# Hyena filter spectra by one radix-2 step, stored once per group, and buffers of their own for the last modulation tiles

## The chip, the cores and the metric

The kernel runs on one core of a Trainium2 chip. The metric is the device time of one execution in microseconds; lower is better. Five engines of the core matter here: TensorE (PE in the profile, its weight loads PEld), VectorE (DVE), ScalarE (ACT), GpSimd (POOL) and SyncE (SP), which here only issues transfers.

## The reference, cut to what matters

Two layers of a diffusion backbone on 256 latent and 256 context tokens of width 2048: an even layer (state-space group and attention group side by side), an odd layer with a Hyena convolution, each with a feed-forward part. Every sub-layer is modulated by vectors that come from `c` (latent) and `c_ctx` (context) through large matrices. The Hyena convolution uses two long filters per channel, which depend on parameters only: a small sine network gives `hid`, and

```python
h_two = jnp.einsum('lf,fkd->lkd', hid, fw_out[:, i]) * window[:, None, :]
k = jnp.concatenate([h_two[:, 0], jnp.zeros((1, d)), jnp.flip(h_two[1:, 1], axis=0)], axis=0)
k = k / jnp.sum(jnp.abs(k), axis=0, keepdims=True)
kf = jnp.fft.rfft(k, axis=0)
uf = jnp.fft.rfft(u, n=2 * seq_len, axis=1)
return jnp.fft.irfft(uf * kf, n=2 * seq_len, axis=1)[:, :seq_len]
```

The kernel computes the spectra `kf` of both filters and the sums of absolute values before anything else, and keeps the spectra in device memory (`kscr`) for the odd layer.

## The kernel before, in words

A TensorE product that must keep full precision is made of three: an operand is cut into a rounded high half (a copy on ScalarE, line 347) and a low half (a subtraction on VectorE, line 348) by `split`, and `mm3` issues high×high, low×high and high×low (lines 380 to 382). Weights come as `raw` tiles of 1 MB and are cut into `whi` and `wlo` in this way.

Only the start of the program is touched. `startup` runs four generators, each of which gives way at every `yield`; `turn` always takes the one whose count of turns, divided by its entry in `START_RATE`, is lowest. Which engine gets what in which order is set by that alone: each engine works off its own queue in program order, and each transfer stands in the queue of the engine that issues it. The four are:

- `filters`: loads the tables, runs the three sine layers (`sin`, `hid`) and forms `hs` and `hd`, the token sums and differences. Then eight groups `gi`: 512 channels of one of the two filters each. A group multiplies by the output weights `fw` (12 products into `pss`), multiplies by the decay window (`sv`, line 762, VectorE), splits that (`sh`, `sl`), takes absolute values (line 766, ScalarE) and their maximum (`am`, line 768), sums over tokens by products with a column of ones (`psl`, 16 of them), and takes a reciprocal into `kinv`. Four blocks of 128 frequencies follow: six `psk` products each over the 256 tokens, an eviction by ScalarE into `ko` (line 785, three buffers of 256 KB) and a store of 256 KB into `kscr`, which ScalarE's own queue issues (line 786).
- `on_pe`: the modulation vectors that layer 0 needs first. 32 tiles `mraw` of 1 MB from `modn` (line 1360), each with eight products into `ps_mod`; after each four tiles a copy `row`, eight small transposing products `ps_modT`, and short column work on VectorE (`mcol`, `mctx`, lines 1375 and 1378) with the scaling of `x` and `cin` (line 1383).
- `stats(0)` and `stats(1)`: loads of the latent and the context tokens, sums of squares (ScalarE, then accumulation on VectorE, line 498) and the reciprocal norm.

When `filters` is through, its pool is closed, the `act` tile is laid out, and `halves` forms the normed inputs (lines 1431 and 1432, `act`) of the four column groups whose modulation is complete. Then the rest of `on_pe`, the first loads of `w_in` (`fetch`, line 352), and layer 0's first projection tasks (`acc` products). The other modulation matrices (`mod`, line 446, 160 tiles) are loaded and used along the whole program: `run` adds to `mod_debt` with each task and loads one tile whenever it reaches 1; VectorE forms each tile's product with `cb` (line 453, 128×2048).

## Time and profile before

| | us |
|---|---|
| median of 3 runs | 2681.16 (2681.15 to 2690.86) |
| profiled execution | 2686.52 |
| its span on the core | 2684.7 |
| mean granted clock of TensorE | 0.992 |

The profiled execution is 5.36 us above the median, and 1.8 us of it lie outside the span. All times of the trace are microseconds from the span's start.

### The profile page before, as it was taken

How to read it: one execution, taken by the hardware profiler on the slowest of the kernel's cores; microseconds unless marked ns; L12 is line 12 of the kernel's file. 1: busy time of each engine (PE TensorE's matmuls, PEld its weight loads, DVE VectorE, ACT ScalarE, POOL GpSimd, SP SyncE). 2: the span in 40 equal slices, each digit the busy share in tenths (PEclk: the TensorE clock that was granted, in tenths of full speed). 3: DMA queues.
4: the chain of work that ended last, by engine and by line, in shares of the span. 5: the costliest groups of instructions: out<-in, count | busy, mean ns of one | idle time of the engine just before them, and what ended most of it. 6: DMA issues, size and time to landing. Idle time of an engine off the chain costs nothing.

```text
span 2684.7 us, 39715 instructions
## 1 busy us (share of the span) xinstructions
PE 2621.0 (98%) x15320; PEld 2241.7 (83%) x15320; DVE 2070.8 (77%) x3137; ACT 1438.6 (54%) x2313; POOL 0.9 (0%) x10
## 2 busy tenths in 40 slices
PE   5999999999999999999999999999999999999998
PEld 2557778988898888888888888888988888888887
DVE  6458776967798888887989999998888656656656
ACT  4463564656564544444546755555654544544545
POOL 0000000000000000000000000000000000000000
PEclk9999999999999999999999999999999999999999
DMA  8776546746578988887887554555578654655543
GB/s 330 271 263 236 197 165 218 260 144 249 205 289 309 334 309 297 320 330 282 341 314 283 199 179 167 189 183 211 205 284 286 211 188 162 215 174 188 201 157 129
DMA packets 108861, 635.88 MB, mean 237 GB/s; under 512 B 11648, under 2 KB 20224, under 8 KB 48256
## 3 DMA queue, kind: packets, MB, share of 16 engines
q1 hardware_dynamic: 104064, 624.95, 64.9%
q10 hardware_dynamic: 4608, 8.39, 0.8%
q8 instruction: 121, 1.98, 0.3%
q14 instruction: 68, 0.56, 0.1%
HBM read 622.81 MB, written 10.49 MB: 236 GB/s over the span
## 4 chain that ended last, share of the span: by engine, by line
PE 89%; DMA 4%; DVE 4%; ACT 1%; issue 1%; SPq 0%; DVEq 0%; ACTq 0%
PE acc L569 40%; PE acc L570 22%; PE acc L813 7%; PE acc L572 3%; PE acc L380 2%; PE acc L381 2%; PE acc L382 2%; DMA mraw<-in_mod 2%; DMA kscr<-ko 1%; PE ps_mod L1363 1%; DVE wlo L348 1%; PE ps_c L380 1%; PE ps_c L382 1%; PE ps_c L381 1%; ACT whi L347 1%
## 5 line engine op out<-in xcount | busy, mean ns | idle before, releaser
L569 PE MATMUL acc<-act,whi 128*128 128x512 f32 x3525 | 1256.8, 396 | 3.0 <-ACT whi L347 3.0
L348 DVE TENSOR_TENSOR wlo<-raw,whi 128x1024 fp32r<-128x1024 f32 (+1 forms) x842 | 937.2, 1118 | 236.3 <-ACT whi L347 229.8
L347 ACT ACTIVATE whi<-raw 128x1024 fp32r<-128x1024 f32 (+1 forms) x842 | 814.3, 972 | 465.4 <-PE acc L569 245.7
L570 PE MATMUL acc<-act,wlo 128*128 128x256 f32 x3760 | 1022.5, 282 | 1.5 <-DVE wlo L348 1.4
L569 PEld LDWEIGHTS acc<-act,whi 128*128 128x128 f32 x3525 | 666.6, 189 | 149.3 <-ACT whi L347 3.8
L570 PEld LDWEIGHTS acc<-act,wlo 128*128 128x128 f32 x3760 | 710.5, 189 | 23.2 <-DVE wlo L348 3.4
L569 PE MATMUL acc<-hh,whi 128*128 128x512 f32 x1280 | 456.5, 395 | 0.0
L453 DVE SCALAR_TENSOR_TENSOR mraw<-mraw,cb 128x2048 f32<-128x2048 f32 x160 | 365.9, 2287 | 44.5 <-DMA mraw<-in_mod 44.1
L570 PE MATMUL acc<-hh,wlo 128*128 128x256 f32 x1408 | 376.8, 282 | 1.1 <-ACT hh L347 0.8
L569 PEld LDWEIGHTS acc<-hh,whi 128*128 128x128 f32 x1280 | 241.0, 188 | 50.7
L570 PEld LDWEIGHTS acc<-hh,wlo 128*128 128x128 f32 x1408 | 265.2, 188 | 13.0 <-ACT hh L347 1.1
L579 ACT ACTIVATE sum<-acc 128x256 f32<-128x256 f32 x160 | 61.3, 383 | 268.8 <-PE acc L572 268.7
L381 PE MATMUL acc<-act,whi 128*128 128x258 f32 (+1 forms) x560 | 160.6, 288 | 5.3 <-DVE act L1432 5.3
L380 PE MATMUL acc<-act,whi 128*128 128x258 f32 (+1 forms) x560 | 161.6, 290 | 2.2 <-ACT whi L347 1.9
L382 PE MATMUL acc<-act,wlo 128*128 128x258 f32 (+1 forms) x560 | 160.8, 287 | 0.1
L813 PE MATMUL acc<-act,whi 128*128 128x512 f32 x480 | 158.1, 408 | 0.0
L582 DVE TENSOR_TENSOR sum<-sum,acc 128x256 f32<-128x256 f32 x203 | 85.0, 419 | 94.7 <-ACT sum L579 94.5
L591 ACT ACTIVATE res<-acc,mcol 128x256 f32<-128x256 f32 x144 | 67.9, 473 | 139.5 <-PE acc L572 136.7
L594 DVE SCALAR_TENSOR_TENSOR res<-acc,mcol,res 128x256 f32<-128x256 f32 x160 | 77.2, 483 | 71.4 <-ACT res L591 57.1
L381 PEld LDWEIGHTS acc<-act,whi 128*128 128x128 f32 x560 | 108.4, 194 | 6.2 <-DVE act L1432 5.7
L380 PEld LDWEIGHTS acc<-act,whi 128*128 128x128 f32 x560 | 108.4, 194 | 2.7 <-ACT whi L347 2.1
L382 PEld LDWEIGHTS acc<-act,wlo 128*128 128x128 f32 x560 | 108.5, 194 | 1.2 <-DVE wlo L348 1.0
(332 smaller groups left out, 2841.1 us busy)
## 6 DMA issues: line engine op xcount, KB each, us to landing
raw<-in_w SPq DMA_DIRECT2D x176, 1024.0 KB, 5.0
mraw<-in_mod SPq DMA_DIRECT2D x160, 1024.0 KB, 5.8
raw<-in_w SPq DMA_DIRECT2D x128, 704.0 KB, 4.3
raw<-in_hw_in SPq DMA_DIRECT2D x48, 1024.0 KB, 4.8
raw<-in_w_in SPq DMA_DIRECT2D x29, 1024.0 KB, 5.0
mraw<-in_modn SPq DMA_DIRECT2D x16, 1024.0 KB, 8.1
mraw<-in_modn SPq DMA_DIRECT2D x32, 512.0 KB, 7.5
raw<-in_w_o SPq DMA_DIRECT2D x16, 1024.0 KB, 4.8
```

What stands on the lines that cost most here:

```text
L347: nc.scalar.activation(hi, src, AF.Copy)
L348: nc.vector.tensor_tensor(lo, src, hi.bitcast(F32), ALU.subtract)
L380: t.matmul(out, lh, rh, start=first, stop=False)
L381: t.matmul(out, lh, rl, start=False, stop=False)
L382: t.matmul(out, ll, rh, start=False, stop=last)
L453: self.nc.vector.scalar_tensor_tensor(raw, raw, 1.0, self.cb, ALU.mult, ALU.mult, accum_out=self.mcol[:, j:j + 1])
L569: t.matmul(*high, start=kt == 0, stop=False, skip_group_check=True)
L570: t.matmul(ps[:, :S], wl, x[:, 0], start=False, stop=False, skip_group_check=True)
L572: t.matmul(*high, start=False, stop=True, skip_group_check=True)
L582: nc.vector.tensor_tensor(v, v, halves[0], ALU.add)
L594: nc.vector.scalar_tensor_tensor(v, halves[0], gate, v, ALU.mult, ALU.add)
L813: t.matmul(ps.rearrange("p (a b) -> p a b", a=2), w, self.act[:, j, :, kt, :S], start=kt == 0 and k == 0, stop=kt == n - 1 and k == 2)
```

## The change

The spectrum of 256 tokens is formed by one radix-2 step. The tokens are put in the order even, odd (in `embT` and `win`, by the host's tables). For each sequence, sum and difference, the even and the odd half are each multiplied by a table of 128 frequencies (`dft_f`, half as wide as `dft_k`, which goes); ScalarE copies the odd half from PSUM (`odd`, one buffer), and VectorE adds it to and subtracts it from the even half into `ko`. So a group has 12 `psk` products in place of 24. `ko` holds a whole group now (128×2048, two buffers) and is stored by one transfer of 1 MB. The two maxima of a group are added on VectorE, and `psl` has 8 products in place of 16. The loads of `fw` and `win` are issued by GpSimd, `win` has two buffers. The filters' own tables are asked for ahead of `cols` and `mats`; `START_AT` goes and `START_RATE` gives the filters 38 in place of 28. The last modulation tiles of `on_pe` get a ring `mring` of three buffers, all of `w_in`'s first three loads are issued ahead of them and cut after every third turn. `mod_debt` starts at −3, so the first three tiles of `mod` come later in the program.

```diff
--- before.py
+++ after.py
@@ -34,8 +34,8 @@
 NFOLD = (4, 4)
 HFOLD = 5
 NSTEP = (4, 1, 4)
-START_RATE = (28, 38, 60, 40)
-START_AT = (1, 0, 0, 0)
+START_RATE = (38, 40, 60, 40)
+MOD_HOLD = 3
 MODS = (1.8, 0.6, 0.68, 0.08, 0.6)
 TICKS = ((1, 1, 1), (1, 2), (4,))
 WAITS = (6, 5, 5, 1)
@@ -119,14 +119,6 @@
     return 2.0 * np.pi * ((t[:, None] * (2 * f[None, :] + 1)) % 1024) / 1024.0
 
 
-def _dft_filter():
-
-    t, f = np.arange(S), np.arange(P)
-    a, b = _dft_angles(t, f), _dft_angles(t, 255 - f)
-    m = np.concatenate([np.cos(a), np.cos(b), -np.sin(a), np.sin(b)], axis=1)
-    return m.reshape(2, P, 512).transpose(1, 0, 2).astype(np.float32)
-
-
 def _dft_forward():
 
     f = np.arange(P)
@@ -161,13 +153,14 @@
     f = lin(1e-4, bands - 1, bands)[None, :]
     fw = (f * w).astype(f32)
     emb = np.concatenate([t, np.cos(fw), -np.sin(fw)], axis=-1).astype(f32)
+    order = np.concatenate([np.arange(0, S, 2), np.arange(1, S, 2)])
     embT = np.zeros((P, S), f32)
-    embT[:HY_EMB] = emb.T
+    embT[:HY_EMB] = emb[order].T
     lo = math.log(1.5) / 1e-2
     hi = math.log(0.3) / 1e-2
     deltas = np.abs(lin(lo, hi, D))
     win = np.exp((-t * deltas[None, :]).astype(f32)).astype(f32)
-    win = win.reshape(2, P, 4, 512).transpose(2, 1, 0, 3)
+    win = win[order].reshape(2, P, 4, 512).transpose(2, 1, 0, 3)
     return embT, np.ascontiguousarray(win)
 
 
@@ -218,7 +211,6 @@
     a["pick"] = np.tile(np.eye(32)[:, :2], (4, 1))
     a["mats"] = _const_mats()
     a["rope"] = _rope_tables()
-    a["dft_k"] = _dft_filter()
     a["dft_f"] = _dft_forward()
     a["dft_i"] = _dft_inverse()
     embT, win = _filter_tables()
@@ -278,7 +270,7 @@
         self.dbg = dbg or {}
         self.bg = []
         self.modq = []
-        self.mod_debt = 0.0
+        self.mod_debt = -float(MOD_HOLD)
         self.mod_landed = []
         self.mod_at = 32
         self.step = 0
@@ -705,14 +697,14 @@
         nc, a = self.nc, self.a
         hidw = pool.tile([P, 3 * P], F32, name="hidw")
         nc.sync.dma_start(hidw, a["hidw"])
-        embT = pool.tile([P, S], F32, name="embT")
+        embT = pool.tile([P, S], F32, tag="hid", name="embT", bufs=2)
         nc.sync.dma_start(embT, a["embT"])
-        nc.sync.dma_start(self.mats, a["mats"])
         rawf = self.wraw.tile([P, KT * P], F32, tag="raw", name="raw_dftf")
-        nc.sync.dma_start(rawf[:, :1024], a["dft_k"].rearrange("p a b -> p (a b)"))
-        fh = pool.tile([P, 2, 512], F32R, name="fh0")
-        fl = pool.tile([P, 2, 512], F32R, name="fl0")
-        self.split(fh.rearrange("p a b -> p (a b)"), fl.rearrange("p a b -> p (a b)"), rawf[:, :1024])
+        nc.sync.dma_start(rawf[:, :512], a["dft_f"].rearrange("p a b -> p (a b)"))
+        fh = pool.tile([P, 2, 256], F32R, name="fh0")
+        fl = pool.tile([P, 2, 256], F32R, name="fl0")
+        yield
+        self.split(fh.rearrange("p a b -> p (a b)"), fl.rearrange("p a b -> p (a b)"), rawf[:, :512])
 
         h = embT
         for j in range(3):
@@ -739,13 +731,13 @@
         for gi in range(8):
             g, i = gi // 2, gi % 2
             fwr = pool.tile([P, 512], F32, tag="fwr", name=self.nm("fwr"), bufs=2)
-            nc.sync.dma_start(fwr, a["fw"][i, g])
+            nc.gpsimd.dma_start(fwr, a["fw"][i, g])
             fwh = pool.tile([P, 512], F32R, tag="fwh", name=self.nm("fwh"), bufs=2)
             fwl = pool.tile([P, 512], F32R, tag="fwl", name=self.nm("fwl"), bufs=2)
             self.split(fwh, fwl, fwr)
             if i == 0:
-                wt = pool.tile([P, 2, 512], F32, tag="win", name=self.nm("win"), bufs=1)
-                nc.sync.dma_start(wt, a["win"][g])
+                wt = pool.tile([P, 2, 512], F32, tag="win", name=self.nm("win"), bufs=2)
+                nc.gpsimd.dma_start(wt, a["win"][g])
             s2 = []
             am = []
             for w, hx in ((0, hs), (1, hd)):
@@ -768,22 +760,28 @@
                 nc.vector.tensor_tensor(amt, two[0], two[1], ALU.max)
                 am.append(amt)
                 yield
+            nc.vector.tensor_tensor(am[0], am[0], am[1], ALU.add)
             ps = self.ps.tile([P, 512], F32, tag="ms", name=self.nm("psl"))
             for ct in range(4):
-                for tt in range(2):
-                    nc.tensor.matmul(ps[:, ct:ct + 1], am[tt][:, ct * P:(ct + 1) * P], self.mat("ones")[:, 0:1],
-                                     start=tt == 0, stop=tt == 1)
+                nc.tensor.matmul(ps[:, ct:ct + 1], am[0][:, ct * P:(ct + 1) * P], self.mat("ones")[:, 0:1],
+                                 start=True, stop=True)
             nc.vector.reciprocal(self.kinv[:, i * 16 + g * 4:i * 16 + g * 4 + 4], ps[:, 0:4])
-            for f, (c0, w) in enumerate(((0, 0), (128, 0), (256, 1), (384, 1))):
-                tag = ("ms", "acc")[f % 2]
-                ps = self.ps.tile([P, 512], F32, tag=tag, name=self.nm("psk"), bufs=3)
-                for tt in range(2):
-                    sl_ = slice(c0, c0 + P)
-                    self.mm3(ps, (fh[:, tt, sl_], fl[:, tt, sl_]), (s2[w][0][:, tt], s2[w][1][:, tt]),
-                             tt == 0, tt == 1)
-                ko = pool.tile([P, 512], F32, tag="ko", name=self.nm("ko"), bufs=3)
-                nc.scalar.activation(ko, ps, AF.Copy)
-                nc.scalar.dma_start(self.kscr[gi][:, f * 512:(f + 1) * 512], ko)
+            ko = pool.tile([P, 4 * 512], F32, tag="ko", name=self.nm("ko"), bufs=2)
+            for w in range(2):
+                two = []
+                for tt in (1, 0):
+                    ps = self.ps.tile([P, 512], F32, tag=("acc", "ms")[tt], name=self.nm("psk"), bufs=3)
+                    r = slice(w * P, (w + 1) * P)
+                    self.mm3(ps, (fh[:, tt, r], fl[:, tt, r]), (s2[w][0][:, tt], s2[w][1][:, tt]), True, True)
+                    two.append(ps)
+                odd = pool.tile([P, 512], F32, tag="odd", name=self.nm("kodd"), bufs=1)
+                nc.scalar.activation(odd, two[0], AF.Copy)
+                for f, op in ((0, ALU.add), (1, ALU.subtract)):
+                    f4 = 2 * w + f
+                    nc.vector.tensor_tensor(ko[:, f4 * 512:(f4 + 1) * 512], two[1], odd, op)
+                if w == 0:
+                    yield
+            nc.scalar.dma_start(self.kscr[gi], ko)
             yield
 
 
@@ -1336,7 +1334,6 @@
         nc.sync.dma_start(cT, a["cT"])
         pick = sp.tile([P, 2], F32, name="pick")
         nc.sync.dma_start(pick, a["pick"])
-        nc.sync.dma_start(self.cols, a["cols"])
         c32 = sp.tile([P, KT, 32], F32, name="c32")
         nc.vector.memset(c32, 0.0)
         nc.scalar.activation(c32[:, :, 0:2], cT, AF.Silu)
@@ -1345,8 +1342,8 @@
 
         def mod_part(q):
 
-            if q % 2 == 0:
-                raw = self.wraw.tile([P, 4, 512], F32, tag="raw", name=self.nm("mraw"))
+            if self.mring is not None or q % 2 == 0:
+                raw = (self.mring or self.wraw).tile([P, 4, 512], F32, tag="raw", name=self.nm("mraw"))
                 return [(raw, 0, 4)]
             return [(self.whl.tile([P, 2, 512], F32, tag=("whi", "wlo")[h], name=self.nm("mraw")), 2 * h, 2)
                     for h in range(2)]
@@ -1404,10 +1401,15 @@
             norm[w] = r
 
         todo = []
+        self.mring = None
         with self.pool(name="filt", bufs=1) as fp:
             gens = [self.filters(fp), on_pe(), stats(0), stats(1)]
-            done = list(START_AT)
+            done = [0] * 4
             live = [True] * 4
+            next(gens[0])
+            nc.sync.dma_start(self.cols, a["cols"])
+            next(gens[2])
+            nc.sync.dma_start(self.mats, a["mats"])
 
             def turn():
                 i = min((k for k in range(4) if live[k]), key=lambda k: done[k] / START_RATE[k])
@@ -1432,11 +1434,20 @@
                         nc.vector.scalar_tensor_tensor(n[1][:, kt, :S], x, sh, n[0][:, kt, :S].bitcast(F32), ALU.add, ALU.subtract)
             todo.clear()
 
-        halves()
-        while any(live):
-            turn()
+        with self.pool(name="mring", bufs=3, side="right") as self.mring:
             halves()
-        self.fetch([(a["w_in"][i], KT) for i in (3, 4, 0)], -1, 3)
+            first = [(a["w_in"][i], KT) for i in (3, 4, 0)]
+            self.landed = [self.load(*w) for w in first]
+            self.loaded = 3
+            n = 0
+            while any(live):
+                turn()
+                halves()
+                n += 1
+                if n % 3 == 0 and self.landed:
+                    self.ready.append(self.split_w(*self.landed.pop(0)))
+                    self.halved += 1
+            self.fetch(first, -1, 3)
         nc.sync.dma_start(self.cb, a["cvec"])
         nc.scalar.activation(self.cb, self.cb, AF.Silu)
```

Three places in the queues. The first is a filter group. ScalarE's queue in the sixth group (stored to `kscr_80`; `kodd` is the copy of the odd half), before:

```order
L785 ACTIVATE ko_1056<-psk_1049 128x512
L785 ACTIVATE ko_1066<-psk_1059 128x512
L786 DMA kscr_80<-ko_1056 128x512
L786 DMA kscr_80<-ko_1066 128x512
L785 ACTIVATE ko_1076<-psk_1069 128x512
L786 DMA kscr_80<-ko_1076 128x512
L785 ACTIVATE ko_1086<-psk_1079 128x512
L786 DMA kscr_80<-ko_1086 128x512
L1366 ACTIVATE row_1239<-ps_mod_1108 128x512
L347 ACTIVATE sh_1123<-sv_1131 128x512
```

and after the change, the same group:

```order
L339 ACTIVATE sh_888<-sv_924 128x512
L339 ACTIVATE sh_890<-sv_932 128x512
L339 ACTIVATE whi_1303<-raw_1283 128x1024
L758 ACTIVATE sv_924<-sv_924 128x512
L758 ACTIVATE sv_932<-sv_932 128x512
L339 ACTIVATE whi_1307<-raw_1283 128x1024
L778 ACTIVATE kodd_962<-psk_954 128x512
L778 ACTIVATE kodd_982<-psk_974 128x512
L339 ACTIVATE sh_997<-sv_1005 128x512
L784 DMA kscr_80<-ko_953 128x2048
L339 ACTIVATE sh_999<-sv_1013 128x512
```

Four evictions, each with a store behind it, become two copies and one store, which now stands behind the next group's first `sh`; two `whi` copies of a tile of `w_in` (`raw_1283`) have come in between.

VectorE's queue at the end of a group, from the last maximum on (the last `sv` belong to the next group), before:

```order
L768 TENSOR_TENSOR am_1029<-sv_1015,sv_1023 128x512
L776 RECIPROCAL kinv<-psl_1039 128x4
L1375 TENSOR_TENSOR mcol<-ps_modT_1091,cols 128x4
L1375 TENSOR_TENSOR mctx<-ps_modT_1091,cols 128x4
L1378 SCALAR_TENSOR_TENSOR mcol<-mcol,cols 128x4
L1378 SCALAR_TENSOR_TENSOR mctx<-mctx,cols 128x4
L1383 SCALAR_TENSOR_TENSOR x_112<-x_112,mcol,rstd_321 128x256 x4
L1383 SCALAR_TENSOR_TENSOR cin_115<-cin_115,mctx,rstd_360 128x256 x4
L762 TENSOR_TENSOR sv_1131<-pss_1127,win_1121 128x512
L762 TENSOR_TENSOR sv_1139<-pss_1135,win_1121 128x512
L348 TENSOR_TENSOR sl_1124<-sv_1131,sh_1123 128x512
```

and after:

```order
L760 TENSOR_TENSOR am_823<-sv_809,sv_817 128x512
L763 TENSOR_TENSOR am_797<-am_797,am_823 128x512
L768 RECIPROCAL kinv<-psl_834 128x4
L1372 TENSOR_TENSOR mcol<-ps_modT_855,cols 128x4
L1372 TENSOR_TENSOR mctx<-ps_modT_855,cols 128x4
L781 TENSOR_TENSOR ko_840<-psk_845,kodd_849 128x512 x2
L754 TENSOR_TENSOR sv_896<-pss_892,win_773 128x512
L754 TENSOR_TENSOR sv_904<-pss_900,win_773 128x512
L781 TENSOR_TENSOR ko_840<-psk_866,kodd_870 128x512 x2
L340 TENSOR_TENSOR sl_889<-sv_896,sh_888 128x512
L340 TENSOR_TENSOR sl_891<-sv_904,sh_890 128x512
```

The addition of the maxima (line 763) and the two pairs into `ko` (line 781) are new; the next group's `sv` stand between the pairs.

The second place is the end of the startup. SyncE's queue before (`mraw<-in_modn` are `on_pe`'s tiles, halves of 128×1024 or whole; `mraw<-in_mod` are those of the later matrices):

```order
L1360 DMA mraw_1423<-in_modn 128x1024
L1360 DMA mraw_1450<-in_modn 128x2048
L1360 DMA mraw_1456<-in_modn 128x1024
L1360 DMA mraw_1457<-in_modn 128x1024
L1360 DMA mraw_1464<-in_modn 128x2048
L1440 DMA cb<-in_cvec 128x2048
L1360 DMA mraw_1470<-in_modn 128x1024
L1360 DMA mraw_1471<-in_modn 128x1024
L352 DMA raw_1503<-in_w_in 128x2048
L352 DMA raw_1505<-in_w_in 128x2048
L352 DMA raw_1539<-in_w_in 128x2048
L446 DMA mraw_1549<-in_mod 128x2048
```

and after:

```order
L1357 DMA mraw_1219<-in_modn 128x1024
L1357 DMA mraw_1220<-in_modn 128x1024
L344 DMA raw_1283<-in_w_in 128x2048
L344 DMA raw_1285<-in_w_in 128x2048
L344 DMA raw_1287<-in_w_in 128x2048
L344 DMA raw_1466<-in_w_in 128x2048
L1357 DMA mraw_1289<-in_modn 128x2048
L1357 DMA mraw_1295<-in_modn 128x2048
L1357 DMA mraw_1329<-in_modn 128x2048
L1357 DMA mraw_1335<-in_modn 128x2048
L1357 DMA mraw_1341<-in_modn 128x2048
L1357 DMA mraw_1355<-in_modn 128x2048
```

Four loads of `w_in` now stand ahead of the last six tiles of `modn`, the first tile of `mod` and `cb` behind or elsewhere.

The third is SyncE's queue ahead of layer 0's output projection, from behind the first load of `w_o`, before:

```order
L446 DMA mraw_5396<-in_mod 128x2048
L446 DMA mraw_5408<-in_mod 128x2048
L352 DMA raw_5476<-in_w_o 128x2048
L446 DMA mraw_5399<-in_mod 128x2048
L446 DMA mraw_5402<-in_mod 128x2048
L446 DMA mraw_5405<-in_mod 128x2048
L446 DMA mraw_5411<-in_mod 128x2048
L446 DMA mraw_5414<-in_mod 128x2048
L352 DMA raw_5423<-in_w_o 128x2048
```

and after:

```order
L438 DMA mraw_5249<-in_mod 128x2048
L438 DMA mraw_5261<-in_mod 128x2048
L438 DMA mraw_5273<-in_mod 128x2048
L438 DMA mraw_5252<-in_mod 128x2048
L344 DMA raw_5390<-in_w_o 128x2048
L438 DMA mraw_5255<-in_mod 128x2048
L438 DMA mraw_5258<-in_mod 128x2048
L438 DMA mraw_5264<-in_mod 128x2048
L438 DMA mraw_5267<-in_mod 128x2048
L438 DMA mraw_5270<-in_mod 128x2048
L438 DMA mraw_5276<-in_mod 128x2048
L344 DMA raw_5285<-in_w_o 128x2048
```

Ten tiles of `mod` stand between the first and the third load of `w_o` where seven stood.

## Rows read from the trace of the kernel before

**Rows 1.** The page, busy time of each engine over the span: us, share, instructions.
```profile
PE 2621.0 (98%) x15320; PEld 2241.7 (83%) x15320; DVE 2070.8 (77%) x3137; ACT 1438.6 (54%) x2313; POOL 0.9 (0%) x10
```

**Rows 2.** TensorE's waits from 214 us: line, releaser; us in total, times, longest.
```profile
PE acc L569 <- ACT whi L347: 3.0, 2, 2.1
```

**Rows 3.** Table by stretches: length, busy us of each engine, PEclk, DMA share, GB/s.
```profile
0.00:50.00 50.00, 23.75 (x77) 7.62 (x78) 29.57 (x71) 22.51 (x50) 0.20 (x4) 0.97 0.97 381
42.80:62.20 19.40, 17.95 (x85) 11.29 (x85) 14.57 (x27) 9.41 (x16) 0.00 (x0) 0.94 0.64 238
62.20:188.90 126.70, 118.85 (x601) 70.49 (x600) 62.00 (x123) 59.53 (x99) 0.19 (x2) 0.96 0.81 273
110.50:132.90 22.40, 19.66 (x87) 10.72 (x86) 7.62 (x15) 7.68 (x13) 0.00 (x0) 0.85 0.76 277
152.80:166.90 14.10, 13.53 (x64) 8.03 (x59) 6.80 (x13) 7.42 (x13) 0.00 (x0) 1.00 0.86 293
188.90:214.00 25.10, 18.77 (x108) 17.55 (x106) 22.82 (x47) 17.84 (x39) 0.00 (x0) 0.73 0.53 181
```

**Rows 4.** Waits from 60 to 190 us, all engines (columns as in rows 2).
```profile
ACT ko L785 <- DMA kscr<-ko: 27.2, 6, 5.8
...
DVE sl L348 <- ACT sh L347: 13.0, 7, 3.2
```

**Rows 5.** The chain of waits up to 220 us: start us, us, what.
```profile
107.27 8.58 DMA kscr<-ko
...
173.68 6.30 DMA raw<-in_w_in
```

**Rows 6.** VectorE's timeline: start us, us, instruction, idle before and releaser.
```profile
24.75 0.53 DVE L691 TENSOR_SCALAR sin<-psh,cols 64x256 f32<-64x256 f32 x1
...
42.82 0.69 DVE L762 TENSOR_TENSOR sv<-pss,win 128x512 f32<-128x512 f32 x1 [0.44 <-PE pss L382]
```

**Rows 7.** Instructions by shape to 215 us: busy us, mean ns; idle before.
```profile
L762 DVE TENSOR_TENSOR sv<-pss,win 128x512 f32<-128x512 f32 x32 | 21.2, 688 | 9.5 <-PE pss L382 9.1
...
L498 DVE TENSOR_TENSOR acc<-acc,sq 128x256 f32<-128x256 f32 x30 | 12.0, 420 | 1.5
...
L768 DVE TENSOR_TENSOR am<-sv,sv 128x512 f32<-128x512 f32 x16 | 11.0, 688 | 15.6 <-ACT sv L766 15.5
...
L348 DVE TENSOR_TENSOR wlo<-raw,whi 128x1024 fp32r<-128x1024 f32 x6 | 7.2, 1221 | 1.3 <-ACT whi L347 1.3
...
L1441 ACT ACTIVATE cb<-cb 128x2048 f32<-128x2048 f32 x1 | 1.9, 1914 | 0.0
```

**Rows 8.** TensorE's timeline in the group from 94.7 us.
```profile
95.15 0.95 PE L1370 MATMUL ps_modT<-pick,row 128*128 128x2 f32 x8
96.03 1.06 PE L1363 MATMUL ps_mod<-mraw,c 128*32 128x512 f32 x8
...
97.36 0.40 PE L381 MATMUL pss<-fwl,hs 128*128 128x512 f32 x1
97.59 0.40 PE L382 MATMUL pss<-fwh,hs 128*128 128x512 f32 x1
```

**Rows 9.** Transfers from 60 to 200 us: count, KB each, median us to landing.
```profile
mraw<-in_modn SPq DMA_DIRECT2D x10, 1024.0 KB, 7.1
...
kscr<-ko ACTq DMA_DIRECT2D x31, 256.0 KB, 6.4
raw<-in_w_in SPq DMA_DIRECT2D x3, 1024.0 KB, 5.5
```

**Rows 10.** VectorE's timeline in the tail.
```profile
197.67 2.29 DVE L453 SCALAR_TENSOR_TENSOR mraw<-mraw,cb 128x2048 f32<-128x2048 f32 x1 [2.11 <-DMA mraw<-in_mod]
```

**Rows 11.** SyncE's list of transfers ahead of layer 0's output projection.
```profile
601.45 25.47 SPq L446 DMA_DIRECT2D mraw<-in_mod  x5
```

**Rows 12.** TensorE's waits from 585 to 660 us.
```profile
PE acc L570 <- DVE wlo L348: 0.6, 1, 0.6
```

**Rows 13.** TensorE's timeline in the group from 110.5 us.
```profile
117.09 0.79 PE L380 MATMUL psk<-sh,fh 128*128 128x512 f32 x1 [2.64 <-ACT sh L347]
```

## The prediction

> **What bounds the kernel now.** The page first: TensorE is busy 98% of the span [rows 1]. Its list of waits from 214 us to the end comes next; it has seven lines that sum to 10.6 us, and the longest line is 3.0 us [rows 2]. So what is won or lost before 214 us moves the whole of the rest, one to one, and the startup is the place to read. The table by stretches shows it: in the seven filter groups after the first, 62.2 to 188.9 us, VectorE is busy 62.0 of 126.7 us and TensorE 118.9 [rows 3]. TensorE's share there is an overlap of pipelined products, and I don't take it for a limit: the one group that nothing stalls, 152.8 to 166.9, takes 14.1 us, while the mean is 126.7/7 = 18.1. The waits say what makes the difference. ScalarE waits 27.2 us in six waits for the store of a spectrum tile to land before it may write a ko buffer again, and behind it in its queue stand the sh copies, for which VectorE waits 13.0 us [rows 4]. The chain of waits runs through those stores (one piece is 8.58 us) and, near the end, through a load of w_in of 6.30 us [rows 5].
>
> **The change part by part.** Profiled time of before: 2686.5 us, of which the span is 2684.7; the median of three runs is 2681.2, that is 5.3 below. I sum differences and take them from the median.
>
> (a) *Filters first.* Before, the sine chain begins at 24.75 us, behind twenty accumulations of squares, and the first product with the window is at 42.82 [rows 6]: 18.1 us, into which ten accumulations at 0.42 us [rows 7] are mixed, so about 14 bare. Now hidw, embT and the half-size DFT table are asked for first; with cols that is 0.9 MB, at the 381 GB/s of the first 50 us [rows 3] some 2.4 us, plus the start of the queue and landing about 12 us in all, so group 0 starts near 26 to 27: 16 earlier. But the 24 or so accumulations that lay ahead of it now lie in it: 24 × 0.42 = 10 back. Its 12 fewer spectrum products at 0.23 to 0.24 us [rows 8] save 3. Group 1 then begins 16 − 10 + 3 = 9 us earlier: **−9**. Bounds: −14 if half of the accumulations find gaps, −4 if the arrivals are 5 us later.
>
> The first 50 us moved data on 97% of all the transfer engines' time [rows 3], so the 1 MB that fw (two tiles) and win bring on GpSimd's queue at the start takes its time from something; I leave it in the bound of −4. The Trainium skill says in "DMA: Bandwidth & Descriptors", section "Issuing engines are not separate DMA queues": another issuing engine saves only issue time, on the same engines. By that rule the 1 MB comes ahead of or between the sine chain's own 0.9 MB, about 2.7 us at the row's rate, and the sum would be 2669. The row agrees on the saturation; whose bytes are served first it doesn't show.
>
> (b) *Groups 1 to 7.* Removed: ScalarE's wait for stores, since a group now has one ko tile of two, and a store has a whole group to land (median 6.4 us for 256 KB [rows 9]; four times the bytes still lie within 14 us). Also two of four evictions on ScalarE. Added to VectorE: one maximum sum at 0.69 us and four add/subtract pairs at the 0.69 us of a PSUM-fed product of the same size [rows 7] = 3.45 us a group. VectorE had 62.0/7 = 8.86 a group [rows 3], so 12.3 now. What cycle follows from 12.3? The page shows two dense stretches of VectorE: group 0 with 14.57 of 19.4 us (75%) and the tail with 22.82 of 25.1 (91%) [rows 3]. At 91% a group takes 13.5 us, at 75% 16.4; the middle, 83%, is 14.8, and I take it, because the group has a fixed chain (pss, sv, sh, sl, psk, and now odd, then ko) and the modulation products between. That is 7 × 14.8 = 103.6. On top comes what the phase did not hold before or does not overlap: two wlo splits at 1.22 us [rows 7] of the w_in tile that is now cut between turns (2.4); ScalarE's wait for that tile, 6.3 in before's chain [rows 5], of which I let 6 stand; the SiLU of the modulation table on ScalarE, 1.9 [rows 7]; and the last group's ko pair and half of another, which have nothing behind them to hide them (3 × 0.69 = 2.0). Sum 12.3. So 115.9 against 126.7: **−10.8**. Bounds: 13.5 a group, −20; 16.4 a group, 0.
>
> (c) *Tail, from the last ko on.* Before it takes 25.1 us to 214 [rows 3], with a modulation product of 2.29 us and its 2.1 us wait for a load [rows 10] in VectorE's queue, and TensorE waits behind it for act tiles. Those go. New: the three-buffer ring lies in the filters' memory, so its second load waits for the last store to land (6.4), then the sixth tile waits until the third is used, hence two loads in a row at 7.1 [rows 9]; column work and its transposes 1.7 (0.95 for the transposes [rows 8] and a few short ones); eight act tiles at 0.42; and a quarter of the two first tasks, 24 products of half width at 0.12 us = 2.8. 6.4 + 14.2 + 1.7 + 3.3 + 2.8 = 28.4 against 25.1: **+3.3**. At the 5.5 us of w_in's loads [rows 9] for all three, 16.5 + 7.8 = 24.3, and −1; at 8 us each +7.
>
> (d) *Three modulation tiles later.* They must be in before layer 0's output projection, where SP's list shows five such loads in 25.5 us [rows 11] ahead of w_o's, and TensorE waits 0.6 us [rows 12]. Three more products at 2.29 us [rows 10] are 6.9 us of VectorE ahead of w_o's buffers. Against no wait at all (0) and all of it (+7) I take **+2**, as the loads before them start sooner.
>
> At nothing: the reordered tokens (tables only); cols and mats after the first yields (mats is first read by psl, far later); eight fewer psl products (TensorE has gaps already).
>
> Sum: −9 − 10.8 + 3.3 + 2 = −14.5. 2681.2 − 14.5 = 2666.7, **2667 us**; the profiled execution would be at 2672.
>
> **The rivals.** 0.5% of 2681 is 13.4 us, about what can be told from no change; the line for faster is 2667.8.
>
> *VectorE less tight.* If the cycle is 13.5 and half of the 12.3 hides, (b) is 94.5 + 6 = 100.5, −26; with the rest 2681 − 30 = 2651. For it: group 6's 14.1 us holds VectorE work of only 6.80 us [rows 3], so waits, not work, make most of a cycle. Against: ko pairs, odd and the next sv are now in each other's way.
>
> *VectorE takes the gain back.* 16.4 a group or more, (b) = 0: 2681 − 9 + 3.3 + 2 = 2677. For it: a sum on VectorE in four places of the chain, in front of the next group's sv; one odd buffer, so the second copy waits for the first pair.
>
> *TensorE's clock falls, slower.* In the group from 110.5 the granted clock is 0.85 [rows 3]: after a wait of 2.64 us for sh, products of 512 columns take 0.79 us in place of 0.40 [rows 8, 13], the lower level of 1.2 GHz. Now a group gives TensorE less: 24 products at 0.24, 32 modulation ones at 1.06/8, 16 small at 0.12 = 11.9 us of 14.8, at half clock 23.8, so that TensorE would become the limit, 9 us a group more. Two such groups undo the gain, a little over three cost 0.5% beyond it; with four it is 2667 + 36 = 2703. Against: before, the clock was 0.96 over the seven groups [rows 3] in spite of ScalarE's six stalls of up to 5.8 us [rows 4]. The Trainium skill, "TensorE: Matmul & The Clock Gate", section "HAM oscillation — how this bites in real kernels", describes this shape: waits between bursts, each next burst begun slow. By it every group could pay, and then seven × 9 = 63 us would come on top; the trace agrees for one group in seven.
>
> **How the numbers follow.** Forecast case (2659 to 2674) 0.44; less tight 0.22; taken back 0.25; slower clock 0.06; else 0.03. Faster: 0.22 and some 0.6 of 0.44 = 0.48. Slower 0.07. Same 0.45. Range: from below the less tight case to the outer bounds of (c) and (d) on the taken-back one, 2648 to 2684.
>
> **What would show it.** VectorE's first product of group 1 at 53 us (58 or later: (a) wrong); of the next groups at a pitch of 14 to 16; no wait of ScalarE for kscr; VectorE near 80% from 53 to 169; the last ko at 169; TensorE's first two tasks done at 197, without a wait from then on; near 640 us a wait of 2 us for w_o. I am wrong if ScalarE's 27 us comes back as VectorE's wait for odd or psk, if the ring's loads hold act past 195, or if the granted clock in the groups is under 0.9.

## The result and the profile after

The changed kernel takes 2699.3 us (median of 6 runs, 2693.4 to 2704.5) against 2682.7 us before (6 runs beside them): ratio 1.0052, 95% interval 1.0035 to 1.0069. It is slower by half a per cent, where 2667 was forecast and the range ended at 2684. The profiled execution has a span of 2696.1 us, 11.4 more than before.

The table by stretches of the changed kernel: start, group 0, the seven other groups, and from the last ko to `ps_dup`, small products that follow layer 0's first tasks (columns as in [rows 3]).

```profile
0.00:50.00 50.00, 21.93 (x99) 10.43 (x100) 36.29 (x89) 24.72 (x56) 4.06 (x11) 1.00 0.97 387
28.51:50.86 22.35, 15.83 (x85) 8.59 (x85) 20.93 (x49) 15.70 (x35) 0.54 (x1) 1.00 1.02 413
50.86:195.40 144.54, 101.50 (x425) 62.19 (x428) 86.46 (x155) 53.38 (x85) 2.87 (x7) 0.77 0.58 217
195.40:241.40 46.00, 37.64 (x216) 27.26 (x209) 27.16 (x59) 22.75 (x46) 0.00 (x0) 0.79 0.60 222
```

The filters start at 28.5 and group 1 at 50.86, 11 us earlier than before. Then the seven groups take 144.5 us in place of 126.7 [rows 3], 20.6 each, with VectorE busy for 60% of it and TensorE's granted clock at 0.77 in place of 0.96. Its waits from 50 to 200 us, in us in total, times, longest:

```profile
PE psl L766 <- DVE am L763: 36.3, 7, 7.5
ACT kodd L778 <- PE psk L374: 33.2, 8, 5.0
```

ScalarE's 27 us of waits for stores [rows 4] are gone; no line of the list names `kscr`. In their place TensorE waits 36.3 us, in each group once, with `psl` for the sum of the maxima, and ScalarE 33.2 us for `psk` products. TensorE's timeline in one group shows what stands behind it:

```profile
77.64 0.39 PE L374 MATMUL psk<-sh,fl 128*128 128x512 f32 x1
...
82.87 1.83 PE L766 MATMUL psl<-mats,am 128*128 128x1 f32 x8 [4.84 <-DVE am L763]
84.56 0.77 PE L372 MATMUL psk<-sh,fh 128*128 128x512 f32 x1
85.14 0.63 PE L373 MATMUL psk<-sl,fh 128*128 128x512 f32 x1
...
87.27 0.63 PE L372 MATMUL pss<-fwh,hs 128*128 128x512 f32 x1
```

The six `psk` behind `psl` need the `sl` of the second half, whose subtraction on VectorE starts thus:

```profile
79.32 1.29 DVE L340 TENSOR_TENSOR sl<-sv,sh 128x512 fp32r<-128x512 f32 x2
...
82.03 0.69 DVE L763 TENSOR_TENSOR am<-am,am 128x512 f32<-128x512 f32 x1
```

That ends at 80.6, and they begin at 84.56: `psl` stands ahead of them in TensorE's queue and waits until the second maximum and the sum are done. And what comes after the wait runs slow: 0.63 to 0.77 us for 512 columns in place of 0.40 [rows 8], the level of 1.2 GHz, until 88.1. The next group's `pss`, from which its chain starts, stand behind all of that. The order of TensorE's queue in one group, by the names of its products (without the modulation ones):

```
before: pss (4 x 3), psk x6, psl x1, psk x13 to x17, psl x7, rest of psk, next pss
after:  pss (4 x 3), psk x6, psl x4, psk x6, next pss
```

(Each `psl` of the queue is two rows in the trace.) Before, one `psl` stood ahead of most `psk` and it needed the first half's maximum only.

The end of the startup: SyncE's list, its waits from 130 us, TensorE's waits after 190 us, and the transposing products of the modulation (first and last start).

```profile
140.18 39.50 SPq L344 DMA_DIRECT2D raw<-in_w_in  x4
189.98 21.29 SPq L1357 DMA_DIRECT2D mraw<-in_modn  x6
```

```profile
SPq L1357 <- DMA kscr<-ko: 9.1, 1, 9.1
SPq L1357 <- DVE am L763: 8.2, 1, 8.2
```

```profile
PE ps_mod L1360 <- DMA mraw<-in_modn: 9.9, 2, 7.6
```

```profile
L1367 PE MATMUL ps_modT<-pick,row x64: 166/251/374, 43.4 to 224.4; 128*128 128x2 f32 x64
```

Four loads of w_in are issued over 39.5 us, the last at 179.4 when its buffer is free. The first of the six tiles of modn behind them leaves at 190.0, after a wait for the last group's `am` and `psl`: its ring lies in the filters' memory. The second leaves at 199.5, when the last store has landed. The last transposes are at 224.4; in the kernel before they are at 190.5. From the last ko to `ps_dup` it takes 46.0 us, before 226.5 − 188.9 = 37.6.

Further on the two traces differ in two places. From the first to the last `ps_o` of the attention it is 86.6 us (577.3 to 663.9) against 79.5 (564.0 to 643.5). From the last high×high `ps_u` of the Hyena layer to the last `psn` product it is 843.3 (1840.6 to 2683.9) against 851.9 (1821.5 to 2673.4). In all: −11.3 (start), +17.8 (groups), +8.4 (tail), −1.6 to the attention, +7.1 in it, −1.3, and −8.6 at the end, which is 10.5 of the 11.4.

### The profile page after: what moved, and what is told of

Its sections match the earlier page's. It is cut to its first block, busy times and chain, and to the rows that moved or that the text cites. A ratio compares the mean times of both kernels' runs of the same rounds, so it can differ in the third digit from the quotient of the medians.

```text
span 2696.1 us, 39384 instructions
## 1 busy us (share of the span) xinstructions
PE 2595.9 (96%) x15160; PEld 2226.9 (83%) x15160; DVE 2093.9 (78%) x3177; ACT 1431.0 (53%) x2297; POOL 7.5 (0%) x22
## 4 chain that ended last, share of the span: by engine, by line
PE 94%; DVE 3%; ACT 2%; DMA 1%; issue 0%; SPq 0%; DVEq 0%; ACTq 0%
PE acc L561 41%; PE acc L562 23%; PE acc L811 6%; PE acc L564 3%; PE acc L372 3%; PE acc L373 3%; PE acc L374 3%; PE ps_mod L1360 1%; PE ps_c L372 1%; PE ps_o L1178 1%; PE ps_c L374 1%; PE ps_c L373 1%; PE ps_y L1056 1%; PE ps_y L1059 0%; PE psl L766 0%
```

## The experiments

All ratios are to the kernel before on the same chip, with a 95% interval. Theory A is that of the order (psl holds up TensorE), B that VectorE's added work sets the cycle, C that the clock is the larger part, T that of the tail's loads. Figures of the groups come from one profiled execution each; two kernels whose groups are the same program (experiment 7) took 123.0 and 120.2 us for the seven, so less than some 3 us is not read as a difference. In the diffs, `...` stands for code left out, and words behind `#` tell what else the edit does.

**1. psl behind psk.** The changed kernel with one block moved:

```diff
             nc.vector.tensor_tensor(am[0], am[0], am[1], ALU.add)
-            ps = self.ps.tile(..., name=self.nm("psl"))
-            for ct in range(4): nc.tensor.matmul(ps[:, ct:ct + 1], am[0]..., ...)
-            nc.vector.reciprocal(self.kinv..., ps[:, 0:4])
             ko = pool.tile(...)
             ...  # psk, odd and the pairs
+            ...  # the lines taken out above
             nc.scalar.dma_start(self.kscr[gi], ko)
```

> The only edit to the changed kernel: the four psl products and the reciprocal stand behind a group's psk products and ko pairs instead of ahead of half of them. Theory A (TensorE's in-order queue: psl, which must wait for the sum of the two maxima, holds up six psk products and the next group's pss): the cycle of a group falls from 20.6 us by some 4 to 5 us to about 16, TensorE's 36 us of waits for am are gone, and the time falls by 28 to 35 us, to 2664 to 2671. Theory B (VectorE's 3.45 us more a group set the cycle): the order of TensorE changes little, under 7 us. Theory C (the fall of TensorE's clock after a wait is the larger part, whatever it waits for): the wait for sh and sl of the second half stays, so the clock in the groups stays under 0.85 and less than 15 us come back.

0.9960 (0.9946 to 0.9974), 2677.6 us, in a comparison in which the kernel before had 2686.6; against the changed kernel's 1.0052 that is 0.9% or 25 us, a little under A's 28 to 35. The groups:

```profile
54.33:174.60 120.27, 99.42 (x421) 55.02 (x420) 85.44 (x155) 53.02 (x85) 2.87 (x7) 0.84 0.66 252
```

17.2 us each in place of 20.6, with the same work on every engine, so A holds and B does not explain these 24 us. The cycle is not down to A's 16. Of C, the clock stays under 0.85 as it said, but more than its 15 us came back, so its main claim falls. In the profiled execution, the slowest of the six, 3.7 of the 24 us were lost in group 0 and 2.6 in the tail. `psl` now waits 1.86 us in the group shown, 7.5 in all seven, and the six `psk` are ahead of it:

```profile
84.06 1.05 PE L781 MATMUL psl<-mats,am 128*128 128x1 f32 x8 [1.86 <-DVE am L763]
84.98 0.48 PE L372 MATMUL pss<-fwh,hs 128*128 128x512 f32 x1
```

**2. The sum of the maxima undone.**

```diff
-            nc.vector.tensor_tensor(am[0], am[0], am[1], ALU.add)
...
-                nc.tensor.matmul(ps[:, ct:ct + 1], am[0]..., start=True, stop=True)
+                for tt in range(2):
+                    nc.tensor.matmul(ps[:, ct:ct + 1], am[tt]..., start=tt == 0, stop=tt == 1)
```

> The only edit to the changed kernel: the maxima are not added on VectorE; psl has 16 products again, two for each column. In the queue of TensorE one psl then stands ahead of the last six psk, as it did before the change, and the other fourteen behind them, among the next group's pss. Theory A: nearly the same gain as with psl put last, 20 to 35 us, so to 2664 to 2680, although TensorE has 64 products more. Theory B: 0.69 us less on VectorE a group, 5 us less in all. Theory C: below 15 us.

1.0001 (0.9990 to 1.0013): 0.5% less than the changed kernel, some 14 us, below A's 20 and within C's 15. The groups take 127.8 us, 18.3 each, at a clock of 0.83. A's direction is borne out, its size is not; why this is 1.1 us a group behind psl put last was not tested.

**3. The subtraction left out,** in the changed kernel and then in that of experiment 7.

```diff
+        ...  # the two ko tiles are made once, ahead of the groups, and cleared by GpSimd
-                for f, op in ((0, ALU.add), (1, ALU.subtract)):
+                for f, op in ((0, ALU.add),):
```

> The subtraction of each ko pair is left out (half of the spectrum is wrong; the ko tiles are cleared once at the start by GpSimd): VectorE has 1.38 us less in each group, the store is the same. Theory A: the pairs lie behind psk and partly beside the next group's pss, so a group gains 0 to 0.7 us, the time falls by 0 to 5 us. Theory B: 1.4 to 2 us a group, 10 to 14 us. Theory C: as A.

2696.5 us in one run. The groups:

```profile
57.77:185.40 127.63, 94.25 (x413) 58.21 (x405) 76.51 (x141) 53.36 (x85) 2.67 (x5) 0.80 0.62 233
```

They came down to 18.2 us each, more than A or B allowed, with one group alone 7 us shorter. Next to nothing of it arrived. The edit has a side effect: GpSimd clears the ko tiles (3.5 us) ahead of the loads of fw that it issues, and group 1 starts at 57.8 in place of 50.9. And the tail became 55.0 us (last ko 185.4, `ps_dup` 240.4): the last tiles of modn came no sooner, with the last transposes at 223.5.

> The kernel with psl behind psk and the old end of the startup, with the subtraction of each ko pair left out (half of the spectrum is wrong). If VectorE's pairs set the cycle once psl is out of the way: 1.4 to 2.4 us less a group, 10 to 17 us less in all than that kernel, 0.987 to 0.990 of the kernel before. If TensorE's order and clock are all: within 4 us of it, 0.992 to 0.995.

0.9951 (0.9935 to 0.9968), no faster than with the subtraction (0.9938). The groups are 14 us shorter (109.0 against 123.0). Group 1 starts 4.9 us later by the same side effect, and the tail takes 11.9: 47.3 against 35.4 us. Here the modulation's last transposes stand at 174.1, at 172.5 with the subtraction. So the time is near the second forecast, though the groups did what the first one said.

**4. Products that nothing reads,** sixteen or four, ahead of psl in each group of the changed kernel.

```diff
+            for _ in range(16):
+                nc.tensor.matmul(ps, fh[:, 0, 0:P], s2[0][0][:, 0], start=True, stop=True)
             for ct in range(4):
```

> Sixteen products of 512 columns (3.8 us at full clock) that nothing reads are put on TensorE ahead of the psl products of each group. It has more work, and fewer and shorter waits; by this the psl products also come to stand behind the psk products. Theory A: the order gives 28 to 35 us as above, the sixteen products take back what of their 3.8 us does not fall into waits, 0 to 2 us a group: 2664 to 2685. Theory B: no gain, or 5 to 25 us slower. Theory C: the clock in the groups comes to 0.95 or more and the time falls by more than with psl last alone, below that kernel's by 5 us or more.

> Four products that nothing reads ahead of psl in each group, in place of the sixteen of the run before; the order of TensorE's queue is otherwise nearly the same, psl behind psk. TensorE has 12 x 0.23 = 2.8 us less to do in a group. If the clock costs nothing here: groups of 15 to 16 us and 15 to 20 us less than with sixteen (2687), or none if the twelve lay in waits. If the sixteen were paid for by the clock that they held up: the granted clock in the groups falls from 0.95 to 0.85 and the groups take as long as with sixteen, 17 to 18 us, within 5 us of 2687.

2687.2 and 2681.4 us, one run each, beside kernels before of 2686.6 and 2684.8. The groups, with sixteen and then with four:

```profile
57.86:182.50 124.64, 113.94 (x527) 66.39 (x525) 84.50 (x156) 52.72 (x85) 2.87 (x7) 0.95 0.67 243
```

```profile
55.86:175.70 119.84, 101.85 (x449) 58.08 (x448) 84.67 (x155) 53.05 (x85) 2.86 (x7) 0.86 0.67 252
```

2.8 us more work a group (twelve products at the 0.23 us of [rows 8]) cost 0.7 us of cycle, while the clock rose from 0.86 to 0.95. That is between the two sharp forecasts, and the 4.8 us that it makes in seven groups are not far above the scatter; waits and the higher clock share the other 2.1 us, and this pair can't divide them. C's claim for the sixteen (5 us or more below psl last) fails, and so does B's, that they gain nothing.

**5. The tail as it was,** in the changed kernel: no ring, w_in's first loads behind the last tiles of modn.

```diff
-        with self.pool(name="mring", bufs=3, side="right") as self.mring:
-            ...  # w_in's loads, then the turns, with a cut of w_in after every third
+        halves()
+        while any(live):
+            turn()
+            halves()
+        self.fetch([(a["w_in"][i], KT) for i in (3, 4, 0)], -1, 3)
```

> The changed kernel with the end of the startup as it was: no ring of its own, the last modulation tiles go into the weights' buffers, w_in's first loads follow them. The groups are left as changed. Theory T (the ring lies in the filters' memory, so the last six tiles of modn are loaded only when the filters are done, and the three loads of w_in ahead of them hold up SyncE's list): these loads move back beside the filter groups, and from the last ko to ps_dup it takes about 37 us as before the change, in place of 46: 8 us less, 2691. Rival: the loads only compete with the groups' own work then, the groups grow by as much, and the time stays within 3 us.

1.0010 (1.0000 to 1.0020), 0.4% or 11 us less than the changed kernel. Groups 144.0 us, unchanged, and 35.0 us from the last ko to `ps_dup`. T holds, and the rival (competition in the groups) falls: the transfer engines' share in the groups only goes from 0.58 to 0.64. The edit takes away the ring and w_in's place ahead of it together; that the ring's place in the filters' memory is what held the tiles is read from SyncE's waits (8.2 and 9.1 us above), not from an experiment.

**6. MOD_HOLD at 0.**

```diff
-MOD_HOLD = 3
+MOD_HOLD = 0
```

> The changed kernel with MOD_HOLD at 0, so that the three modulation tiles are loaded in the first tasks as before; nothing else differs. If their later place costs what the two traces show around the attention (first to last ps_o 79.5 us before, 86.6 after), 5 to 7 us come back there, and the first tasks lose at most 2: about 2693. Rival: the 7 us are of that execution or of another order of tasks; then the time stays within 2 us.

1.0083 (1.0068 to 1.0098), slower than the changed kernel by 0.3%, with intervals that just touch. The attention is back at 79.5 us as expected, but the end of the program is at 854.0 in place of 843.3 and the startup's end 3.5 us later. There the first tile of `mod` has come into the last filter group, where VectorE waits 1.2 us for it and multiplies for 2.3, ahead of two of that group's `sv`. The rival falls as well: in all eleven traces with MOD_HOLD 3 the attention takes 85.2 to 86.6 us and the end 843.3 to 843.7, in the four with 0, the kernel before among them, they take 79.5 to 79.6 and 851.3 to 854.0. So both belong to the three tiles, and they give back at the end more than they cost in the attention.

**7. psl last and the old tail,** with MOD_HOLD 3 and 0: the edits of 1 and 5, then of 6 too.

> psl behind psk, and the end of the startup as it was, MOD_HOLD 3. If the two causes add: groups 120 us, tail about 38 in place of 48.6, so 10 us below the kernel with psl last alone, near 0.992 of the kernel before. If the loads only move the wait into the groups: no better than psl last alone, 0.996.

> As the kernel with psl behind psk and the old end of the startup, and MOD_HOLD at 0 too: what is left of the change is the radix-2 step, the group stores, the sum of the maxima and the queue and order of the start. If all three causes add, another 5 to 7 us less, 0.990 of the kernel before; if the three tiles cost nothing where they are, the same as with MOD_HOLD 3.

0.9938 (0.9920 to 0.9956), 2670 us, and 0.9948 (0.9933 to 0.9963). The groups of the first:

```profile
51.61:174.60 122.99, 105.74 (x485) 57.37 (x483) 82.90 (x160) 53.03 (x86) 2.87 (x7) 0.85 0.76 289
```

By the stages the causes A and T add up: `ps_dup` comes at 210.0, at 223.2 with psl last alone. In the time it is 0.2% below psl last alone, and those two intervals overlap. With MOD_HOLD 0 there is no difference that the intervals show; by stages it is 79.6 against 85.5 us in the attention, 851.7 against 843.4 at the end, and 120.2 against 123.0 in the groups, at a clock of 0.91.

**8. The radix-2 step alone,** put into the kernel before (tables, pairs on VectorE, one store a group; the rest as before).

```diff
-            ...  # four times six psk, an eviction by ScalarE into ko, a store of 256 KB
+            ...  # psk, odd, the pairs into one ko and one store, as in the changed kernel
```

> The kernel before with the radix-2 step and the group's one store alone: order of the start, queues, psl with 16 products, end of the startup and MOD_HOLD are as before. ScalarE's 27 us of waits for stores go, VectorE gets 2.76 us more a group. Theory: the two are about even, the cycle stays at 17 to 19 us and the time within 7 us of the kernel before (0.997 to 1.003). If the waits for stores were the groups' limit, as the prediction has it: 0.990 to 0.995. If VectorE's pairs are worse than these waits: above 1.004.

1.0021 (1.0008 to 1.0034). ScalarE waits for no store any more, and yet:

```profile
65.75:201.40 135.65, 117.94 (x523) 66.62 (x522) 83.99 (x160) 53.49 (x86) 0.19 (x2) 0.80 0.70 264
```

19.4 us a group, 1.3 more than before, at a clock of 0.80. Group 0 is 4.4 us longer too and the tail 6.7 shorter (30.9 us), so 0.2% are left. The time is in the first range and the cycle just above it; a gain from the waits for stores, as the prediction has it, does not appear.

**9. All but the radix-2 step:** the kernel of 7 with MOD_HOLD 3, with the wide table and 24 psk again, and ScalarE's evictions into the group's ko.

```diff
-            ...  # two psk of 128 tokens each, odd and a pair, for each half
+            for f, (c0, w) in enumerate(((0, 0), (128, 0), (256, 1), (384, 1))):
+                ...  # six psk products into one tile, as before
+                nc.scalar.activation(ko[:, f * 512:(f + 1) * 512], ps, AF.Copy)
```

> The kernel with psl behind psk and the old end of the startup, with the radix-2 step itself taken out: the wide table and 24 psk products a group, four evictions by ScalarE, no odd copy and no pair on VectorE; the group's ko tile of 128x2048 and its one store stay, win has one buffer again. Against the kernel with psl behind psk and the old end (2670, 17.6 us a group): theory B' (what is left in a group is VectorE's, and TensorE, with less to do, falls to the lower clock): the cycle falls to 14 to 15.5 us, the granted clock in the groups is 0.95 or more, and the time is 14 to 24 us lower, 0.985 to 0.989 of the kernel before. Rival: the 12 products fewer are worth what they take, 2.8 us a group: 10 to 20 us slower, 0.998 to 1.001.

0.9926 (0.9908 to 0.9944), 2665.6 us, the lowest of all and below both kernels; it can't be told from the 0.9938 with the step. It lies between the two forecasts: the clock is where B' had it, the cycle and the time are not. The groups take 16.1 us each, at a clock of 0.98, and the tail 41.4 us:

```profile
52.58:165.10 112.52, 106.53 (x522) 61.19 (x521) 65.54 (x123) 57.69 (x97) 3.39 (x8) 0.98 0.83 300
```

**10. The same, evicted by VectorE,** to part VectorE's work from TensorE's clock.

```diff
-                nc.scalar.activation(ko[:, f * 512:(f + 1) * 512], ps, AF.Copy)
+                nc.vector.tensor_tensor(ko[:, f * 512:(f + 1) * 512], ps, s2[w][0][:, 0].bitcast(F32), ALU.add)
```

> The kernel without the radix-2 step (psl behind psk, old end of the startup, 24 psk a group), but the four evictions of a group are additions on VectorE instead of copies on ScalarE (each adds the rounded high half of a filter tile, so the spectrum is wrong). VectorE then has as much to do in a group as with the radix-2 step, TensorE as much as without it. If VectorE's four instructions are what makes a group of the radix-2 kernel longer (17.6 against 16.1 us): 17 us or more a group, VectorE near 83 us busy in the seven, and the time at 0.994 of the kernel before or above. If it is the lower clock of a TensorE with half of the products (0.85 against 0.98): the groups stay at 16.1 to 16.6 us, the clock at 0.96 or more, the time near 0.9926.

```profile
56.95:165.50 108.55, 101.71 (x496) 60.00 (x495) 80.12 (x151) 42.19 (x68) 3.21 (x6) 0.98 0.75 278
```

0.9954 (0.9941 to 0.9968). In the groups it is the second answer: VectorE busy for 80 us, and still 15.5 us a group at a clock of 0.98. In the time it is the first: group 0 takes 28.9 us in place of 24.9 and the tail 48.5 in place of 41.4. So VectorE's four instructions don't lengthen the seven groups here; by the stages the edit costs 11 us around them and gains 4 in them, 7 in all, at the edge of what the two intervals show. It takes as much from ScalarE as it gives to VectorE: ScalarE is busy for 42 us, for 53 with the radix-2 step, so it doesn't show what a group does with the work of both.

## Why the prediction was wrong

**(a), the start: right**, with parts that came out otherwise: −11.3 against −9. The sine chain begins at 10.5 us, 12 was counted, and the filters at 28.5, 26 to 27 was forecast. The chain takes 18.0 us as before, not 14: eight accumulations lie in it again, and in the kernel before there were seven and not the ten that were taken off. Group 0 then grew by 3 us in place of 7. The first 50 us moved 387 GB/s against 381 [rows 3] with two queues issuing, so the row agrees with the rule that the prediction takes from the Trainium skill ("DMA: Bandwidth & Descriptors", section "Issuing engines are not separate DMA queues").

**(b), the groups: this step failed**, by 28.6 us (+17.8 against −10.8). Its removal was right: ScalarE's wait went, and VectorE's work came out at 86.5/7 = 12.4 us, 12.3 forecast. What failed first is a term put at nothing. The prediction spoke of psl only as eight products fewer; but the new sum is one more link ahead of psl, and psl stands ahead of half of psk and of the next pss in TensorE's queue. Moving it gave 24 us in the groups and 25 in the time (experiment 1). The Trainium skill states the rule that this hangs on, "PSUM — Partial Sum Buffer", section "Engine vs sequencer instructions": matrix products start and complete in program order. The trace agrees, with `psk` held from 80.6 to 84.56 us. The second is "What cycle follows from 12.3?": a share of VectorE between 75 and 91% was taken from two dense stretches and laid over a group whose cycle is a chain through three engines. The share was 60%, and 71% with psl last, where the groups take 120.3 us, 4.4 more than the 115.9 forecast.

Third, the radix-2 step itself gives no shorter group: 19.4 against 18.1 alone (experiment 8), 17.2 to 17.6 against 16.1 with psl last (7 and 9). VectorE's sum of work alone is not what makes them longer: nearly as much of it without the step leaves them at 15.5, though with less on ScalarE (10). Yet without the subtraction a group of the radix-2 kernel is some 2 us shorter (3). So it can be the place of the pairs, in a chain by way of the one odd buffer, for which ScalarE waits 10.9 us in the groups of 7 and 18.3 in those of 8, or TensorE's clock of 0.80 to 0.91 in place of 0.96 to 0.98; these two were not parted, and the cause of this part stays open.

**(c), the tail: right in mechanism, mis-sized**: +8.4 against +3.3. The ring's second tile did wait for the last store to land, as counted; it left 4.1 us behind the last ko, 6.4 was counted. What was too small are the two loads in a row, 14.2: from the second tile's issue at 199.5 to the last product with a tile of modn at 222.3 there are 22.8 us. TensorE waits for that tile until 204.5, and from 210.8 on it works, without a wait, on layer 0's first tasks, between which the products of the last three tiles stand.

**(d): right in the attention, at its upper bound, and incomplete.** +7.1 in the attention: VectorE has 6.3 us more to do in it, and TensorE stands idle for 3.1 us at a clock of 0.96 in place of 1.00. The −8.6 at the end was not looked for, and it comes with the three tiles too (experiment 6). In the 190 us behind the Hyena layer TensorE stands idle for 4.8 us at a clock of 0.98 in the kernel before, and for 4.3 to 6.0 us at 0.97 to 0.98 in the three other traces with MOD_HOLD 0; in the changed kernel it waits for nothing there, at 1.00. So the term came to −1.5 in place of +2. What the later tiles change in that stretch was not followed further.

**The rivals.** The slower one ended nearest: 2703 was its price with four slow groups, 2699 came. That is luck in part: its sign, TensorE at half clock after a wait, is in the trace in every group, but its trigger was named wrongly (sh in place of psl), and the clock alone is not the larger part: with psl last it is still 0.84, yet 24 us are gone. It had 0.06 because I argued from the clock of 0.96 that held with twice the products, and from one slow group in seven. There was a second: in the kernel before, the first `pss` of group 2 (76.1 to 78.8 us) run at 0.63 us too. "VectorE takes the gain back" has its number refuted; of its reasons, VectorE's sum of work is not borne out (10) and the one odd buffer stays open. "Less tight" has its number refuted too, but its reason, that waits and not work make most of a cycle, is what the groups show. Of the signs of being wrong that the prediction named, the clock under 0.9 came (0.77); ScalarE's wait came back, but as TensorE's for the sum of the maxima and ScalarE's own for psk, which were not among them.

**"Moves the whole of the rest, one to one": not so for the groups.** A shorter filter phase isn't a shorter startup. In experiment 3 the groups gave 17 and 14 us and the time nothing: 6.9 and 4.9 us went to the later start, and 9.0 and 11.9 to the tail, since the end waits for the last of on_pe's tiles. With the old tail `ps_dup` comes 35 to 40 us behind the last transposes wherever the filters end by then or up to 3 us later (before 36.0, experiment 5 37.5, 9 35.2, 10 39.9); only in experiment 8, whose last ko is 15 us behind them, is it 45.9.

## What to carry to other kernels

An engine's busy share doesn't give a cycle. Write out, for one cycle, what each in-order queue has ahead of the next cycle's first instruction, and move an instruction that waits for the end of a side chain behind everything that is ready. When work is taken from TensorE in a stage that is a chain through several engines, look at what it will wait for then and at its clock after the wait; and before a phase is shortened, find the second one that ends beside it.

## What was not expected of the hardware

Twelve products of 512 columns more in each group, 2.8 us of work that nothing uses, cost 0.7 us a group in one run each: the granted clock went from 0.86 to 0.95. And with half of the `psk` products, and the pairs on VectorE, the groups of the kernel before ran at 0.80 in place of 0.96. The Trainium skill tells of such falls where loads are late ("TensorE: Matmul & The Clock Gate", "HAM oscillation — how this bites in real kernels"); here it is VectorE and ScalarE that TensorE waits for (5.5 us for `sl` and 4.3 for `sh` in the groups of experiment 8).
